# Two small moves on the vector engine in a four-sublayer encoder trunk: the second copy of a gate row, and two gated products

## The chip, the cores and the metric

One NeuronCore of one Trainium2 chip. The time is the device time of one execution in microseconds (us). The kernel before has a median of 1330.57 us over three runs (1330.4 to 1330.78). The engines that matter here: TensorE (PE, matmuls; PEld is its weight load), VectorE (DVE, elementwise work), ScalarE (ACT, copies, casts and activations), GpSimd (POOL, which here issues the DMAs that add into their destination) and the DMA queue that is fed by SyncE (SPq).

## The reference, cut to what matters

Two layers, each of a token mixer and a SwiGLU feed-forward net (FFN), on one sequence of 512 tokens with 1024 features. Every one of the four sublayers has a norm before it and after it, and shift, scale and gate rows from a conditioning vector:

```python
h = rmsnorm(x, norm_g[i, 2]) * (1.0 + scale) + shift
gate, up = jnp.split(h @ w_in, 2, axis=-1)
y = (jax.nn.silu(gate) * up) @ w_out          # w_in 1024 x 5632, w_out 2816 x 1024
x = x + gate_row * rmsnorm(y, norm_g[i, 3])
```

(The last line's `gate_row` is the gate of the conditioning vector, called `gate` in the reference.) All values are float32.

## The kernel before, in words

**Arithmetic.** A float32 operand is split into a high part that TensorE takes in its fp32r format (a cast on ACT) and the remainder (a subtraction on DVE). One product of two tiles is then three matmuls: high by high, high by low and low by high. So every operand tile costs one ACT cast and one DVE subtraction before PE can use it in full.

**Seven products.** The output projection of each FFN is cut into 2 x 2 blocks (tokens in two halves, features in two halves, the inner dimension in even and odd tiles) and computed with seven block products in place of eight; `PRODUCTS` lists for each the result bank (A, B, C, D), the weight block (b11 to b22) and the activation block (a11 to a22, or the sum s1). The sums of weight blocks are made on the way: by DMAs that add (`add_`, issued by POOL) and by DVE. The four results collect in PSUM banks, with A used over and over: when a product has to leave A or has been gathered there, it is copied or combined into an SBUF tile.

**The first FFN** (L1130 to L1271). `seq` lists the steps q; each step is one tile pair of one product: 12 matmuls by `product` (two token tiles x two inner tiles x three). The order on each engine is written out by hand (`manual_schedule`), so an engine takes its instructions in the order of this loop. Behind the matmuls of step q come, in this order: `behind(q)`, which holds copies of finished banks, issues the adding DMAs and makes block differences; then a gate row for q = 0 and 1; then `w_prep(q + 4)`, the split of the weight tile of four steps later (ACT cast L1098, DVE subtraction L1099); then `a_prep(q + 3)`, the split of the activation tile of three steps later (L1107 on ACT, L1108 on DVE) and, for the first two products, one block sum or difference (L1110, L1112). Four weight tiles (`whl_p`) and three activation tiles are in turn.

**Gate rows.** `put_gates(s)` (L310) brings the gate row of sublayer s into DRAM, where the sublayers read it back later, spread over all partitions. It has three steps: a transpose on PE into a PSUM bank `ggp` (L313), a DVE copy of 8 x 128 values into the SBUF tile `gr` (L316), and a DMA of `gr` to `gate_d[s]` on SP's queue (L317). There is a single buffer for `gr`, so a second copy has to wait until the DMA of the first has landed. Rows 2 and 3 are begun together ahead of the step loop (both transposes), and each is finished, copy and DMA, by `list(rows_g[q])` at L1235.

**The last FFN** (L2202 to L2300). The same seven products as 40 steps n. The loop at L2272 runs `products([n])`, then `behind(n)`, then `w_prep(n + 4)` (ACT L1980, DVE L1981) and `a_prep(n + 3)` (ACT L1993, DVE L1994); from n = 34 on, `behind(n)` comes after the two preps. Steps 33 and 27 are run inside the turn of 32 and 26, between `behind(32)` and `behind(33)`, and ahead of the preps. `got["11", t]` is the finished first accumulator (token tile t = 0, 1, first 512 features). Its squares are summed on ACT at n = 29 and 30. `behind(33)` subtracts bank A into `got["22", t]` (L2246), after which A is free for step 34. `behind(34)` takes the square root (ACT, L2215), the reciprocal (DVE, L2216) and multiplies `got["11", t]` by the gate row `gg[0]` (DVE, `gated`, L2219), for t = 0 and 1. `behind(35)` and `behind(36)` do more gated products and write the first outputs (`x_new`, L2225). The last three steps, 37 to 39, run as one group by token tile, and the tail of the kernel squares, gates and writes what is left in bank A. The gate rows `gg` are fetched from `gate_d` at n = 26 (L2283).

Of the kernel before, what the change touches and what calls it, by code (L numbers as in the profile page):

```python
# [38 lines left out]
def trunk_kernel(  # L39
# [540 lines left out]
    with ExitStack() as ph:  # L580
# [571 lines left out]
        with tc.manual_schedule(engines={PE_ENGINE, mybir.EngineType.SP, mybir.EngineType.Activation,  # L1152
                                         mybir.EngineType.DVE, mybir.EngineType.Pool}):
            load_pair(0)
            madds = ada_begin(14)
            for i, f in ((0, 0), (2, 0), (1, 1), (3, 1), (4, 2), (5, 3)):
                rest(i)
                if i in (2, 3):
                    up(f, lead_ps[i])
                    sums(1)  # L1160
                    low_parts()
                else:
                    gate(f, lead_ps[i])
                sums(1)
            finish = out_begin(1, w2, lambda k: acts[k], NF, ggs, xn_lead, "aux", None,
                               lambda: load_w([(wm_in, P, P)]), ys=ys, held=held)[2]
            plain_tiles = finish(())
            tiles = []
            last = 2 * NF - 7
            for k in range(last + 1):  # L1170
                if k % 2 == 0 and k < 2 * NF - 10:
                    load_pair(k // 2 + 1)
                if k in (16, 20, 24):
                    x_load((k - 16) // 4)
                if k in (last - 2, last - 1):
                    xy_load(n_s - 2 + k - last + 2)
                tiles.append(in_chunk(ws[k], h))
                for step in todo:
                    next(step, None)
                q, j = divmod(k - 3, 4)  # L1180
                if j < 2 and k > 2:
                    gate(4 + 2 * q + j, tiles[k - 1])
                elif k:
                    up(2 + 2 * q + j, tiles[k - 1])
                if k + 2 < len(splits):
                    for op in splits[k + 2]:
                        op()
                low_parts()
                sums(4 if j < 2 else 3)
                if k == 2 * NF - 12:  # L1190
                    ggs.append(make_gg(1, gg_tile))
                if k == last - 1:
                    assert next(madds, None) is None and not ada_sets and not quarters
                    sums_p.close()
                    ph.enter_context(tc.tile_pool(name="gap", bufs=1, side="right", reuse_waits="tile")).tile(
                        [P, 216], F32, tag="gap", name="gap")
                    ao_p.append(ph.enter_context(tc.tile_pool(name="aop", bufs=3, side="right", reuse_waits="tile")))
                    ao_p[0].tile([P, 2, 2, 256], F32R, tag="ao", name="ao")
                    gotp = ph.enter_context(tc.tile_pool(name="gotp", bufs=1, side="right", reuse_waits="tile"))
                    c22 = gotp.tile([P, 2, T], F32, tag="c22", name="c22")  # L1200
                if k >= last - 1:
                    w_prep(seq[k - last + 1])
                    a_prep(seq[k - last + 1])
            w_prep(seq[2])
            a_prep(seq[2])
            up(NF - 1, tiles[-1])
            for step in todo:
                list(step)
            rows_g = [put_gates(q, mm_ps) for q in (2, 3)]
            for step in rows_g:  # L1210
                next(step)
            for p in range(n_s - 2):
                y_load(p)
            for p in range(n_s):
                add_(b_("b12", p), b_("b11", p))
            w_prep(seq[3])
            low_parts()
            leads, lead_ops, tail_w = [], [], [[], []]
            tails = ((0, NF - 2), (1, NF - 4), (1, NF - 2))

            def tail_split(i):
                hf, k0 = tails[i]
                w = whl_p.tile([P, 2, 2, T], F32R, tag="whl", name="whlo")
                split_w(plain[hf, k0], w, 2)
                tail_w[hf] += [(k0 + kk, w, kk) for kk in range(2)]

            for q, item in enumerate(seq):
                if item[0] == "s":
                    product(item)
                else:  # L1230
                    w = w_of[item]
                    plain_tiles(item[1], [(item[2] + kk, w, kk) for kk in range(2)], item[3])
                behind(q)
                if q < 2:
                    list(rows_g[q])  # L1235
                if q == 13:
                    plain[1, NS] = plain_load(1, NS, flat_half(s1t, 0))
                    plain[0, NS] = plain_load(0, NS, flat_half(s1t, 1))
                elif q == 24:
                    plain[0, NS + 2] = plain_load(0, NS + 2, flat_half(wx[0], 0))  # L1240
                if q + 4 < len(seq):
                    w_prep(seq[q + 4])
                if q + 3 < len(seq):
                    a_prep(seq[q + 3])
                if q == 27:
                    st_p.close()
                    lead_p.append(ph.enter_context(tc.tile_pool(name="leadp", bufs=16, reuse_waits="tile")))
                    xns += [tile4l([P, 2, T], F32, "xn") for _ in range(4)]
                    for load in ssd_lead[:2]:
                        leads += load(lead_ops)  # L1250
                    for xn, (hf, k0) in zip(xns, tails):
                        plain[hf, k0] = plain_load(hf, k0, xn)
                    for op in lead_ops[:4]:
                        op()
                    leads += ssd_lead[2](lead_ops)
                elif q == 28:
                    for op in lead_ops[4:6]:
                        op()
                    tail_split(0)
                    for op in lead_ops[6:8]:  # L1260
                        op()
                elif q == 29:
                    tail_split(1)
                elif q == 30:
                    tail_split(2)
                    for op in lead_ops[8:10]:
                        op()
                elif q == 31:
                    for op in lead_ops[10:]:
                        op()  # L1270
            begun = finish(tail_w, leads)  # L1271
# [496 lines left out]
    with ExitStack() as ph:  # L1768
# [249 lines left out]
        with tc.manual_schedule(engines={PE_ENGINE, mybir.EngineType.SP, mybir.EngineType.Activation,  # L2018
# [187 lines left out]
            got = {}  # L2206
# [21 lines left out]
            def behind(n):  # L2228

                for t in range(2):  # L2230
                    if n == 5:
                        got["11", t] = t2("c11")
                        act.copy(got["11", t], bank["A"][t])
                    elif n == 10:
                        dve.tensor_add(got["11", t], got["11", t], bank["B"][t])
                    elif n == 16:
                        got["12", t] = t2("c12")
                        act.copy(got["12", t], bank["C"][t])
                    elif n == 21:
                        dve.tensor_add(got["12", t], got["12", t], bank["D"][t])  # L2240
                        got["22", t] = spare[f"c22_{t}"]
                        act.copy(got["22", t], bank["D"][t])
                    elif n == 27:
                        dve.tensor_tensor(got["12", t], got["12", t], bank["A"][t], SUB)
                    elif n == 33:
                        dve.tensor_tensor(got["22", t], got["22", t], bank["A"][t], SUB)  # L2246
                    elif n in (29, 30):
                        if t == n - 29:
                            square(t, 0, got["11", t])
                            square(t, 1, got["12", t])  # L2250
                            mean(t)
                    elif n == 34:
                        root(t)
                        gated(got["11", t], 0, got["11", t])
                    elif n == 35:
                        square(2 + t, 0, got["22", t])
                        mean(2 + t)
                        gated(got["12", t], 1, got["12", t])
                        x_new(t, 0, got["11", t])
                    elif n == 36:  # L2260
                        gated(got["22", t], 1, got["22", t])
                        x_new(t, 1, got["12", t])
# [67 lines left out]
```

## Time and profile before

| | us |
|---|---|
| median of three runs | 1330.57 (1330.4 to 1330.78) |
| the profiled execution's own time | 1330.71 |
| its span, first to last instruction | 1328.9 |
| PE busy, of the span | 1314.1 (99%) |
| DVE busy | 1028.2 (77%) |
| ACT busy | 641.7 (48%) |
| POOL busy | 86.1 (6%) |

The profile's times count from the start of the span. A line of the timeline gives the start, the duration, the engine, the line in the kernel, the operation, what it writes and reads, how many were merged, and in square brackets how long the engine sat idle before it and what ended that idle time. A line of the chain of waits gives start, duration and the engine or transfer on which the end of the kernel hung during that stretch. Instructions of one engine overlap slightly: the next one can begin some 0.1 us before the recorded end of the one before.

### The profile page before, as it was taken

The numbers are of one execution on the slowest core, as the hardware profiler recorded it, in microseconds if no ns is written. First come the engines' busy times: TensorE is split into PE (matmuls) and PEld (weight loads), VectorE is DVE, ScalarE is ACT, GpSimd is POOL, SyncE is SP. The second block draws the span as 40 slices with busy tenths as digits, with TensorE's granted clock in tenths as the row PEclk, the third lists the DMA queues.
The fourth block names the chain that finished last, engine by engine and source line by source line (L and its number), as shares of the span: only waits on it lengthen the run. The fifth ranks groups of instructions, "written<-read, shape, count | busy, mean of one in ns | idle before, by whom it ended". The sixth has DMA issues, their size and how long they took to land.

```text
span 1328.9 us, 19226 instructions
## 1 busy us (share of the span) xinstructions
PE 1314.1 (99%) x7437; PEld 1134.3 (85%) x7437; DVE 1028.2 (77%) x1654; ACT 641.7 (48%) x1042; POOL 86.1 (6%) x106
## 2 busy tenths in 40 slices
PE   8999999999999999999999999999999999999997
PEld 6788889888888788898888888888789999998886
DVE  5588866787776596768998989888677777766897
ACT  5332256222223465665654555554574555554665
POOL 0000000000000140000000000000000111101320
PEclk9999999999999999999999999999999999999999
DMA  9767760788886692414533243413251788869861
GB/s 308 231 193 225 246 229 1 218 265 258 289 285 201 175 171 61 139 34 130 166 121 124 84 138 115 143 64 127 80 158 45 192 216 214 199 191 287 175 124 64
DMA packets 203456, 222.21 MB, mean 167 GB/s; under 512 B 8788, under 2 KB 148964, under 8 KB 202340
## 3 DMA queue, kind: packets, MB, share of 16 engines
q1 hardware_dynamic: 186496, 184.74, 44.7%
q0 software_dynamic: 12720, 23.34, 10.2%
q10 hardware_dynamic: 4148, 12.90, 3.0%
q8 instruction: 58, 0.95, 0.3%
q14 instruction: 34, 0.28, 0.1%
HBM read 195.37 MB, written 2.24 MB: 149 GB/s over the span
## 4 chain that ended last, share of the span: by engine, by line
PE 94%; SPq 2%; DVE 2%; ACT 1%; DMA 1%; issue 1%; DVEq 0%; ACTq 0%
PE ip L279 15%; PE ip L281 14%; PE ip L280 14%; PE y L381 10%; PE sA L1920 7%; PE cA L2015 4%; PE sC L1920 3%; PE cA L1127 3%; PE li L279 3%; PE li L281 3%; PE li L280 3%; PE sB L1920 2%; PE li L767 1%; PE yd L1512 1%; PE cC L2015 1%; PE cB L2015 1%
## 5 line engine op out<-in xcount | busy, mean ns | idle before, releaser
L279 PE MATMUL ip<-h,whl 128*128 128x512 f32 x840 | 331.2, 394 | 0.2 <-DVE cv L874 0.2
L281 PE MATMUL ip<-h,whl 128*128 128x512 f32 x840 | 327.2, 390 | 0.0
L280 PE MATMUL ip<-h,whl 128*128 128x512 f32 x840 | 327.0, 389 | 0.0
L279 PEld LDWEIGHTS ip<-h,whl 128*128 128x128 f32 x840 | 157.8, 188 | 33.8 <-issue 1.8
L281 PEld LDWEIGHTS ip<-h,whl 128*128 128x128 f32 x840 | 157.7, 188 | 33.2
L280 PEld LDWEIGHTS ip<-h,whl 128*128 128x128 f32 x840 | 157.8, 188 | 31.6
L225 DVE TENSOR_TENSOR whl<-wst,whl 128x1024 fp32r<-128x1024 f32 x99 | 120.4, 1221 | 42.2 <-ACT whl L224 42.1
L224 ACT CAST whl<-wst 128x1024 fp32r<-128x1024 f32 x99 | 102.4, 1042 | 57.8 <-DMA wst<-in_f_w_in_dram 47.5
L127 DVE SCALAR_TENSOR_TENSOR ada_acc<-ada_st,csil,ada_acc 128x512 f32<-128x512 f32 x140 | 105.0, 750 | 20.4 <-DMA ada_st<-in_ada_w_dram 17.0
L381 PE MATMUL y<-whlo,ys 128*128 128x512 f32 x384 | 89.4, 392 | 0.0
L381 PEld LDWEIGHTS y<-whlo,ys 128*128 128x128 f32 x384 | 71.7, 188 | 15.9 <-issue 0.7
L279 PE MATMUL li<-h,whl 128*128 128x256 f32 x288 | 83.2, 289 | 0.0
L281 PE MATMUL li<-h,whl 128*128 128x256 f32 x288 | 81.5, 283 | 0.0
L280 PE MATMUL li<-h,whl 128*128 128x256 f32 x288 | 81.5, 283 | 0.0
L1920 PE MATMUL sA<-tq,whl 128*128 128x256 f32 x576 | 74.6, 283 | 0.3 <-DVE g L1946 0.3
L1920 PEld LDWEIGHTS sA<-tq,whl 128*128 128x128 f32 x576 | 71.5, 190 | 0.6 <-DVE g L1946 0.5
L1366 DVE SCALAR_TENSOR_TENSOR cu<-ip,cols,cu 128x511 f32<-128x511 f32 (+2 forms) x84 | 62.7, 747 | 4.0 <-ACT cu L1363 1.4
L2015 PE MATMUL cA<-whlo,ao 128*128 128x512 f32 x264 | 61.2, 390 | 0.8 <-DVE ao L1994 0.4
L2015 PEld LDWEIGHTS cA<-whlo,ao 128*128 128x128 f32 x264 | 49.3, 188 | 12.2 <-ACT whlo L1980 1.2
L1876 DVE TENSOR_TENSOR whl<-wsu,whl 128x1024 fp32r<-128x1024 f32 x33 | 40.4, 1223 | 23.4 <-ACT whl L1875 23.4
L279 PEld LDWEIGHTS li<-h,whl 128*128 128x128 f32 x288 | 55.2, 192 | 0.0
L280 PEld LDWEIGHTS li<-h,whl 128*128 128x128 f32 x288 | 55.2, 192 | 0.0
(371 smaller groups left out, 2319.1 us busy)
## 6 DMA issues: line engine op xcount, KB each, us to landing
ada_st<-in_ada_w_dram SPq DMA_DIRECT2D x96, 512.0 KB, 5.6
wst<-in_f_w_in_dram SPq DMA_DIRECT2D x26, 1024.0 KB, 7.6
wst<-in_m_w_in_dram SPq DMA_DIRECT2D x14, 1024.0 KB, 5.3
wst<-in_m_w_in_dram SPq DMA_DIRECT2D x20, 512.0 KB, 5.7
wst<-in_a_w_in_dram SPq DMA_DIRECT2D x9, 1024.0 KB, 6.9
wsu<-in_f_w_in_dram SPq DMA_DIRECT2D x17, 512.0 KB, 6.0
csb<-cs_d ACTq DMA_DIRECT2D x8, 1024.0 KB, 5.5
sg<-in_f_w_in_dram SPq DMA_DIRECT2D x32, 256.0 KB, 3.3
```

The source lines that it names most:

```text
L127: dve.scalar_tensor_tensor(acc, w, csil[:, k:k + 1], acc, MUL, ADD)
L224: later.append((lambda sw=sw, w=w: act.copy(w[:, 0, :nk, :], sw), lambda sw=sw, w=w: dve.tensor_tensor(w[:, 1, :nk, :], sw, w[:, 0, :nk, : ...
L225: lambda sw=sw, w=w: dve.tensor_tensor(w[:, 1, :nk, :], sw, w[:, 0, :nk, :].bitcast(F32), SUB)))
L279: pe.matmul(dst, w_at(w, 0, kk), a[:, 0, sl], start=start, stop=False)
L280: pe.matmul(dst, w_at(w, 0, kk), a[:, 1, sl], start=False, stop=False)
L281: pe.matmul(dst, w_at(w, 1, kk), a[:, 0, sl], start=False, stop=stop)
L381: pe.matmul(pst, a[:, al, tk], wt[:, wl, kk, :], start=k == 0 and i == 0, stop=k == K - 1 and i == 2, skip_group_check=bool(held))
L1127: pe.matmul(bank[r, sub], a[:, al, q, tk], w[:, wl, q, :], start=first and k == 0, stop=False, skip_group_check=True)
L1366: dve.scalar_tensor_tensor(u[:, sft:], pst[:, :T - sft], w[3 - sft], u[:, sft:], MUL, ADD)
L1876: dve.tensor_tensor(dst[:, 1], src, dst[:, 0].bitcast(F32), SUB)
L1920: pe.matmul(dst, w[:, wl, k0 + k, :], moving(q, k, al), skip_group_check=True, start=q in ("P1", "P5", "P2") and k == 0 and i == 0, stop=k ...
L2015: pe.matmul(bank[r][sub], a[:, al, q, tk], w[:, hl, q, :], start=first and k == 0, stop=last and k == 2, skip_group_check=True)
```

## The change

Two edits, which touch no operand and no result. In the first FFN the second gate row (copy L316 and DMA L317 of row 3) is finished behind step q = 5 in place of q = 1. In the last FFN the two gated products of the first accumulator are issued at n = 31 in place of n = 34; the square roots and reciprocals stay at n = 34.

```diff
@@ first FFN, step loop
                 behind(q)
-                if q < 2:
-                    list(rows_g[q])
+                if q in (0, 5):
+                    list(rows_g[q // 5])
@@ last FFN, behind(n)
                             mean(t)
+                    elif n == 31:
+                        gated(got["11", t], 0, got["11", t])
                     elif n == 34:
                         root(t)
-                        gated(got["11", t], 0, got["11", t])
```

On DVE's instruction stream, row 3's copy (L316) moves from ahead of `w_prep(5)` to ahead of `w_prep(9)`; fourteen DVE instructions lie between. Its DMA keeps its place in SP's queue: no other DMA of that queue lies between the two places. The two products (L2219) move from behind `a_prep(37)` to between `a_prep(33)` (L1994, 128 x 256) and the subtraction of `w_prep(35)` (L1981, 128 x 1024), which is ahead of the two subtractions that free bank A (L2246). Nothing else changes place on any engine. DVE carries out the same number of instructions as before. Of the lines named here only those from L2254 on get other numbers (one more); L2219 and L2246 keep theirs.

## The prediction

> **What bounds the kernel now.** I read the page's table of engines and its chain first, then the chain of waits in order of time around the two places of the change, then the timeline of both places.
>
> ```profile
> PE 94%; SPq 2%; DVE 2%; ACT 1%; DMA 1%; issue 1%; DVEq 0%; ACTq 0%
> ```
>
> The end hangs on PE for 94% of the span. An edit on DVE can only be worth what it does to the few stretches where PE waits. The chain has such a stretch in each of the two places. In the first FFN it reads:
>
> ```profile
> 451.34 2.75 PE cA L1127 x12
> ...
> 456.99 5.35 DMA gate_d<-gr
> 462.36 0.28 DVE gr L316
> 462.64 1.13 DVE whlo L1099
> 463.77 0.61 DVE ao L1108
> 464.43 10.72 PE cB L1127 x46
> 475.15 10.88 PE cC L1127 x48
> ```
>
> The chain leaves PE for the DMA of gate row 2, goes on over the DVE copy of row 3 that waited for it, and comes back to PE by the activation split of step 4. The size of the hole comes from the rate: four steps of 12 matmuls take 10.88 us (the cC row; 0.2267 each). Step 0 began at 451.34, so C should begin 2 x 10.88 later, at 473.10; it begins at 475.15. **PE loses 2.05 us.** The timeline of DVE and ACT there:
>
> ```profile
> 456.88 1.06 ACT L1098 CAST whlo<-w2x 128x1024 fp32r<-128x1024 f32 x1
> 457.85 0.61 ACT L1107 CAST ao<-raw 128x512 fp32r<-128x512 f32 x1
> 458.73 0.69 DVE L1110 TENSOR_TENSOR raw<-s1t,raw 128x512 f32<-128x512 f32 x1
> ...
> 462.36 0.28 DVE L316 COPY gr<-ggp 8x128 f32<-8x128 f32 x1 [2.94 <-DMA gate_d<-gr]
> 462.57 1.20 DVE L1099 TENSOR_TENSOR whlo<-w2x,whlo 128x1024 fp32r<-128x1024 f32 x1
> 463.70 0.67 DVE L1108 TENSOR_TENSOR ao<-raw,ao 128x512 fp32r<-128x512 f32 x1
> ```
>
> DVE sits idle for 2.94 us until the 4 KB of row 2 have landed, although its next split (weight tile 5, L1099) has had its ACT cast since 457.94 and the one after (L1108) since 458.46. PE's first two matmuls of step 4 use high parts only; the third needs that L1108, and waits.
>
> In the last FFN the timeline shows the end of the loop:
>
> ```profile
> 1302.76 0.42 DVE L1994 TENSOR_TENSOR ao<-raw,ao 128x256 fp32r<-128x256 f32 x1
> 1303.10 1.22 DVE L1981 TENSOR_TENSOR whlo<-w2t,whlo 128x1024 fp32r<-128x1024 f32 x1
> 1304.24 0.68 DVE L1994 TENSOR_TENSOR ao<-raw,ao 128x512 fp32r<-128x512 f32 x1
> ...
> 1305.25 1.37 DVE L2246 TENSOR_TENSOR w2h<-w2h,cA 128x512 f32<-128x512 f32 x2 [0.33 <-PE cA L2015]
> ...
> 1306.08 11.62 PE L2015 MATMUL cA<-whlo,ao 128*128 128x512 f32 x50 [0.19 <-DVE w2h L2246]
> ...
> 1309.12 1.15 ACT L1980 CAST whlo<-w2h 128x512 fp32r<-128x512 f32 x2 [1.32 <-PE cA L2015]
> ...
> 1310.81 1.28 ACT L2215 ACT_TABLE_LOAD   x1
> ...
> 1312.10 0.48 ACT L2215 ACTIVATE ss<-ss 128x1 f32<-128x1 f32 x2
> 1312.43 0.17 DVE L2216 RECIPROCAL ss<-ss 128x1 f32<-128x1 f32 x1 [0.40 <-ACT ss L2215]
> 1312.49 0.61 ACT L1980 CAST whlo<-w2h 128x512 fp32r<-128x512 f32 x1
> 1312.51 0.67 DVE L2219 TENSOR_TENSOR c<-c,w2h 128x512 f32<-128x512 f32 x1
> ...
> 1313.10 0.15 DVE L2216 RECIPROCAL ss<-ss 128x1 f32<-128x1 f32 x1
> 1313.17 0.67 DVE L2219 TENSOR_TENSOR c<-c,w2h 128x512 f32<-128x512 f32 x1
> ...
> 1313.76 0.68 DVE L1981 TENSOR_TENSOR whlo<-w2h,whlo 128x512 fp32r<-128x512 f32 x1
> ...
> 1317.62 0.41 DVE L1994 TENSOR_TENSOR ao<-raw,ao 128x256 fp32r<-128x256 f32 x1
> ...
> 1318.09 3.94 PE L2015 MATMUL cA<-whlo,ao 128*128 128x512 f32 x16 [0.39 <-DVE ao L1994]
> ```
>
> PE waits twice: for L2246, which frees bank A for step 34 (1306.08), and for the last activation split (L1994 at 1317.62). By the rate, 50 matmuls from 1306.08 end at 1306.08 + 11.33 = 1317.41, and the next starts at 1318.09: **0.68 us** lost. The two products that move (L2219) lie on DVE ahead of this second wait, and their new place is ahead of the first one.
>
> **The first edit, step by step.** What goes is the 2.94 us wait and the copy. DVE then takes weight tile 5 right behind L1110, at 459.42 (458.73 + 0.69) at the latest; L1099 takes 1.13 to the next start (462.57 to 463.70), so L1108 begins at 460.55 and is done by 461.22. PE's third matmul of step 4 is due at 462.22 + 0.45 = 462.67 (451.34 + 10.88, and two matmuls). So the split is 1.4 us early, and the whole 2.05 goes: **-2.05 us**. What is late next? Nothing at once: a step asks DVE for a weight split (1.13), an activation split (0.67) and a block sum or difference like L1110 (0.69), 2.5 us against PE's 2.72, so the lead grows; the ACT casts of later weight tiles wait for PE to free their buffers and come with it.
>
> What is added, with the next item of SP's queue behind row 3's DMA:
>
> ```profile
> 485.93 5.83 SPq L1083 DMA_DIRECT2D s1t<-in_f_w_out_dram  x2
> ```
>
> The copy comes four steps of 2.5 us behind 459.42, at about 469, and takes 0.21 start to start (462.36 to 462.57) where DVE is ahead by at least that 1.4; the cover gone, it would cost 0.21. It still waits for the DMA of row 2, landed by 462.34, seven us before. The DMA of row 3 goes out about 7 us later than now, 16 us ahead of SP's next item; its reader is in the last FFN (below). I take 0 for copy and DMA.
>
> Weighed against it: the Trainium skill, DMA: Bandwidth & Descriptors, section "Latency and other measured facts", speaks of a DMA's fixed cost of about 2 us. By that alone, an estimate, row 2 would land at 458.99, before DVE could ask, and there would be no wait to remove. This trace differs: 5.35 us.
>
> **The second edit.** Its added part first. In the new place there are two products of 0.59 each from start to next start (1312.51 to 1313.10, 1313.17 to 1313.76): 1.18 us in all, ahead of L1981 at 1303.10. Their gate row is there:
>
> ```profile
> 1263.31 1.10 SPq L2283 DMA_DIRECT2D w2h<-gate_d  x2
> w2h<-gate_d SPq DMA_DIRECT2D x2, 256.0 KB, 4.8
> ```
>
> That is landed by 1270. The only slack up to L2246 is from 1304.84 (L1994 at 1304.24 and 0.60 to the next start) to 1305.25: 0.41. So L2246 comes 1.18 - 0.41 = **0.77 us later**, and PE starts step 34 at 1306.85. Wholly beside other work the pair would cost 0, without slack 1.18; I take 0.77 since both ends of the slack are rows.
>
> Then what it gives back. ACT's casts at 1309.12 wait for PE's step 34, so they, the table load and the square roots behind them all come 0.77 later: roots at 1312.87, first reciprocal at 1313.20, second at about 1313.4, behind the second root's end. The next subtraction (L1981, now 1313.76) needs the cast that moves from 1312.49 to 1313.26 and ends at 1313.87: it starts at about 1313.90. So the 1.18 us taken off DVE here turn into waits for ACT, and the last split comes 0.14 **later**, at 1317.76. PE reaches that point at 1306.85 + 11.33 = 1318.18, and resumes when the split lets it, at 1318.23 in place of 1318.09; everything behind (squares, root, products, the outputs) hangs on this: **+0.14 us**. The bounds: -0.68, the second wait gone and the first not grown; +0.77, nothing given back.
>
> **Sum.** -2.05 + 0.14 = -1.91 us. Against the profiled execution: span 1328.9 to 1326.99, with 1330.71 - 1328.9 = 1.81 around it 1328.80. That execution lies 0.14 above the median, so I take the change from the median: 1330.57 - 1.91 = **1328.7 us**.
>
> **Rivals.**
>
> ```profile
> 1301.62 1.23 DVE L1981 TENSOR_TENSOR whlo<-w2t,whlo 128x1024 fp32r<-128x1024 f32 x1 [1.49 <-ACT whlo L1980]
> ```
>
> *The pair finds room.* If L2246 isn't held up (DVE and PE meet differently at step 33), the second wait goes: -2.05 - 0.68 gives 1327.8. For it: 0.41 of slack and 1.49 us of DVE idle just before 1301.62. Against it: that idle time lies ahead of the pair's place in DVE's order.
>
> *The tail pays in full.* The 0.77 at step 34 stays: -2.05 + 0.77 gives 1329.3. For it: ACT's chain moves with PE. Against it: the 0.68 us hole is there to take it up.
>
> *The first edit doesn't do what it says.* Row 2's DMA is slow only in the profiled execution, and lands ahead of 459.42 in the timed runs, which then have no wait to lose: +0.14 alone, 1330.7. Against it: the profiled execution is 0.14 us, not 2, above the median.
>
> *Starved adds (slower).* In the first FFN, POOL issues the adding DMAs while DVE works:
>
> ```profile
> 462.75 0.86 POOL L1046 DMA_DIRECT2D w2y<-w2x  x1 [1.34 <-DVE gr L316]
> 463.57 0.92 POOL L1046 DMA_DIRECT2D w2s<-w2s  x1
> 464.91 0.87 POOL L1046 DMA_DIRECT2D w2s<-w2s  x1 [0.41 <-issue]
> ...
> 478.56 1.29 DVE L1099 TENSOR_TENSOR whlo<-w2y,whlo 128x512 fp32r<-128x512 f32 x2 [0.52 <-ACT whlo L1098]
> ...
> 480.38 0.68 DVE L1150 TENSOR_TENSOR w2x<-w2y,w2x 128x512 f32<-128x512 f32 x1
> w2y<-w2y POOLq DMA_DIRECT2D x6, 256.0 KB, 4.3
> ```
>
> Three of them were issued from 462.75 on, right as DVE's idle time ended. If POOL can't issue while DVE is busy, they wait for DVE's next hole, the 0.52 us at 478.04, with the new lead 475.99; at 1.34 us each (463.57 to 464.91) the second series starts at 480.0 and its first add lands at about 484.4 (4.3 by the last row). L1150, which reads it, would be due at 478.33: 6.1 late, less the 1.4 of lead 4.7 of PE's time, so 1328.7 + 4.7 = 1333.4. The result is slower than before once that add lands after 481.6 (478.33 + 1.4 + 1.91). Against it: the issues at 463.57 and 464.91 ran beside back-to-back DVE work. By the Trainium skill, SBUF — State Buffer, section "Who interferes with whom", a DVE instruction with two SBUF inputs blocks a GpSimd instruction that reads SBUF, which would speak for this rival; it infers that making descriptors isn't of that kind, and these rows agree.
>
> **How the numbers follow.** Chances: the forecast (1328.3 to 1329.1) 0.63, the pair finds room 0.13, the tail pays in full 0.12, no wait in the timed runs 0.05, starved adds 0.05, else 0.02. 0.2% is 2.66 us, about what a measurement of this kernel can tell from no change: faster is below 1327.91, slower above 1333.23. Faster holds most of the first rival: 0.13. Slower holds most of the starved adds and part of the rest: 0.05. Same: 0.82. The range from 1327.7 to 1329.8 takes in the three likeliest cases.
>
> **What would show it.** Right: no wait of L316 on the DMA; step 4's third matmul directly behind its second, C beginning 10.88 after B; L2246 some 0.77 later against PE's step 33, so that its 0.33 us of idle time is gone; PE's start of step 34 as much later; the hole before the last 16 matmuls gone. Wrong: a new wait in steps 5 to 20 on an adding DMA, on L1099 or L1108; or L2246 not late.

## The result, and the profile after

The kernel after takes 1328.68 us (median of 16 runs, 1328.27 to 1329.71) against 1330.64 us for the kernel before, run beside it (16 runs). The ratio is 0.9984 with a 95% interval of 0.9977 to 0.9992, so the change is faster by 0.16%, inside the bound of 0.2%. The profiled execution took 1328.93 us with a span of 1327.1. Two of those 16 runs of the kernel before took over 1332 us, and in the three sets of runs taken beside the experiments up to nearly half did (its medians there: 1331.03, 1331.64 and 1331.45), so ratios of different sets are not set against each other; what lies behind this is followed below. One run of the experiments took 1446.76 us at a granted clock of 0.85, where all others have 0.996 or more, and is left out.

The chain of waits of the kernel after in the first FFN (start, duration, engine):

```profile
451.31 10.90 PE cA L1127 x48
462.21 10.88 PE cB L1127 x48
473.09 7.03 PE cC L1127 x31
```

No transfer and no vector instruction stands in the chain any more. B begins 10.90 behind A, and C 10.88 behind B: the 2.05 us are gone. The timeline of DVE in the same stretch shows why:

```profile
458.70 0.69 DVE L1110 TENSOR_TENSOR raw<-s1t,raw 128x512 f32<-128x512 f32 x1
459.31 1.22 DVE L1099 TENSOR_TENSOR whlo<-w2x,whlo 128x1024 fp32r<-128x1024 f32 x1
460.44 0.68 DVE L1108 TENSOR_TENSOR ao<-raw,ao 128x512 fp32r<-128x512 f32 x1
...
469.30 0.27 DVE L316 COPY gr<-ggp 8x128 f32<-8x128 f32 x1
```

The split of step 4 (L1108) starts at 460.44 in place of 463.70, and the copy of row 3 at 469.30 has no brackets behind it: it waits for nothing. POOL's timeline, on which the rival of the starved adds rested:

```profile
462.67 0.86 POOL L1046 DMA_DIRECT2D w2y<-w2x  x1 [0.87 <-DMA gate_d<-gr]
463.62 0.86 POOL L1046 DMA_DIRECT2D w2s<-w2s  x1
464.96 0.87 POOL L1046 DMA_DIRECT2D w2s<-w2s  x1 [0.48 <-DVE whlo L1099]
```

The three adds go out at the times of before (462.75, 463.57, 464.91), although DVE now works through the whole stretch. The end of the last FFN, all engines:

```profile
1299.70 1.23 DVE L1981 TENSOR_TENSOR whlo<-w2t,whlo 128x1024 fp32r<-128x1024 f32 x1 [1.49 <-ACT whlo L1980]
...
1300.84 0.42 DVE L1994 TENSOR_TENSOR ao<-raw,ao 128x256 fp32r<-128x256 f32 x1
...
1301.17 1.29 DVE L2219 TENSOR_TENSOR c<-c,w2h 128x512 f32<-128x512 f32 x2
1302.38 1.22 DVE L1981 TENSOR_TENSOR whlo<-w2t,whlo 128x1024 fp32r<-128x1024 f32 x1
...
1304.11 1.28 DVE L2246 TENSOR_TENSOR w2h<-w2h,cA 128x512 f32<-128x512 f32 x2
...
1304.94 15.30 PE L2015 MATMUL cA<-whlo,ao 128*128 128x512 f32 x66 [0.99 <-ACT whlo L1980]
...
1311.30 0.35 DVE L2216 RECIPROCAL ss<-ss 128x1 f32<-128x1 f32 x2 [0.48 <-ACT ss L2215]
...
1311.99 0.69 DVE L1981 TENSOR_TENSOR whlo<-w2h,whlo 128x512 fp32r<-128x512 f32 x1 [0.34 <-ACT whlo L1980]
...
1315.85 0.42 DVE L1994 TENSOR_TENSOR ao<-raw,ao 128x256 fp32r<-128x256 f32 x1
...
1320.28 0.60 ACT L2209 ACTIVATE w2s<-cA 128x512 f32<-128x512 f32 x1 [2.35 <-PE cA L2015]
```

L1994 at 1300.84 stood at 1302.76 before, so this stretch arrives 1.92 us earlier. L2246 stood at 1305.25 and now stands at 1304.11, only 1.14 earlier: the pair ahead of it has cost it 0.78, and its 0.33 us of idle time is used up. PE's 66 matmuls run in one piece, without the hole ahead of the last 16. The profile puts PE's 0.99 us down to an ACT cast; what came last is L2246, whose start lies 0.83 ahead of PE's, as before (1305.25 and 1306.08).

### The profile page after: what moved, and what is told of

The parts are those of the page before. It is cut to its first block, busy times and chain, and to the rows that moved or that the text cites. A ratio compares the mean times of both kernels' runs of the same rounds, so it can differ in the third digit from the quotient of the medians.

```text
span 1327.1 us, 19226 instructions
## 1 busy us (share of the span) xinstructions
PE 1313.8 (99%) x7437; PEld 1134.4 (85%) x7437; DVE 1028.0 (77%) x1654; ACT 641.5 (48%) x1042; POOL 85.9 (6%) x106
## 4 chain that ended last, share of the span: by engine, by line
PE 93%; DMA 2%; SPq 2%; DVE 1%; ACT 1%; issue 1%; DVEq 0%; ACTq 0%
PE ip L279 15%; PE ip L281 14%; PE ip L280 14%; PE y L381 8%; PE sA L1920 7%; PE cA L2015 4%; PE cA L1127 3%; PE sC L1920 3%; PE li L279 3%; PE li L281 3%; PE li L280 3%; PE sB L1920 2%; PE li L767 1%; PE yd L1512 1%; PE cC L2015 1%; PE cD L2015 1%
```

## The experiments

Two theories stood against each other for the first edit. Mine: the wait for the buffer `gr` is the hole. The rival: the hole comes from the place of the copy (the load on DVE in these steps), or is worth something else in the timed runs than in the profile. For the second edit, mine: the pair delays the freeing of bank A by as much as it later frees DVE; the rival: it finds room. Ratios are to the kernel before, run beside each. Since A begins between 450.9 and 452.6 us in different executions, profiles are compared by one distance: from the start of bank A's matmuls in the first FFN to the start of the last square (L2209) in the tail. It is 870.73 us before (the square starts at 1322.07) and 868.97 after. For the second edit a shorter one leaves out what happens ahead of the last FFN: from the weight split of step 34 (L1981, at 1301.62 before and 1299.70 after) to the same square. It is 20.45 us before and 20.58 after.

**The copy alone.** The second hunk of the diff is left out.

> The first edit alone, everything else as before. Theory (the copy's wait for row 2's DMA is the hole in PE; the pair at step 31 costs a little): 2.05 us off, less 0.1 lost again on the way to the end, so 1.9 to 2.05 below the kernel before, about 1328.6; the copy of row 3 at about 469.3 without a wait; cC begins at 473.1; in the last FFN everything stands as before against PE's steps. Rival (the pair finds room, and the first edit is worth less): only 1.2 to 1.4 below, about 1329.3.

Measured: 1328.49 us, ratio 0.9979 (0.9970 to 0.9988); the distance is 868.73, 2.00 less than before, and the shorter distance 20.46 (from 1300.46). Its tail, all engines:

```profile
1304.10 1.37 DVE L2246 TENSOR_TENSOR w2h<-w2h,cA 128x512 f32<-128x512 f32 x2 [0.33 <-PE cA L2015]
...
1304.93 11.60 PE L2015 MATMUL cA<-whlo,ao 128*128 128x512 f32 x50 [0.20 <-DVE w2h L2246]
...
1316.92 3.96 PE L2015 MATMUL cA<-whlo,ao 128*128 128x512 f32 x16 [0.39 <-DVE ao L1994]
```

The two waits of PE stand where they stood before (50 matmuls, a hole, 16). The first edit carries the whole gain.

**The pair alone.** The first hunk is left out.

> The second edit alone. Theory: DVE's L2246 comes 0.77 us later, PE's last 16 matmuls no longer wait, and the end comes 0.14 us later: 1330.8, not to be told from no change by time, but by the rows (L2246 at 1306.0 in place of 1305.25, the last 16 matmuls at about 1318.2). Rival (the pair finds room): 0.68 us earlier, about 1329.9.

Measured: 1331.97 us (median of ten runs), ratio 1.0002 (0.9993 to 1.0011); the distance is 870.97, 0.24 more than before, and the shorter distance 20.57 (from 1301.67), 0.12 more. The tail:

```profile
1306.09 1.27 DVE L2246 TENSOR_TENSOR w2h<-w2h,cA 128x512 f32<-128x512 f32 x2
...
1306.92 15.28 PE L2015 MATMUL cA<-whlo,ao 128*128 128x512 f32 x66 [0.98 <-ACT whlo L1980]
...
1313.24 0.35 DVE L2216 RECIPROCAL ss<-ss 128x1 f32<-128x1 f32 x2 [0.46 <-ACT ss L2215]
...
1317.81 0.41 DVE L1994 TENSOR_TENSOR ao<-raw,ao 128x256 fp32r<-128x256 f32 x1
```

Step 34 starts 0.84 later than before (1306.08), of which 0.05 lies ahead of the pair (L1981 at 1301.67 in place of 1301.62); the hole ahead of the last 16 is gone, and the last split comes at 1317.81 where it came at 1317.62. One wait has become the other.

**The copy at its old place, in a buffer of its own.**

```diff
-        gr = tmp.tile([KD, P], F32, tag="gr", name="gr", bufs=1)
+        gr = tmp.tile([P, 256], F32, tag="uh", name="gr", bufs=2)[:KD, :P] if s == 3 else tmp.tile([KD, P], F32, tag="gr", name="gr", bufs=1)
```

> The kernel before with a second buffer for the gate row (row 3 goes into a tile of another tag that is idle then), both copies in their old places at steps 0 and 1. Theory (the wait for the DMA costs, not the copy's place): the copy of row 3 runs at about 459.3 without a wait, takes its 0.2 us out of the 1.4 us of lead, and PE loses nothing: about 2.0 below the kernel before, 1328.6. Rival (the place counts: DVE work at step 1 is on PE's path): at most the wait less 0.2 and whatever the DMA of row 3 so close behind row 2's adds, 1.5 or less gained, 1329.1 or more.

Measured: 1328.31 us, ratio 0.9980 (0.9971 to 0.9989), distance 868.68. DVE's timeline:

```profile
458.94 0.27 DVE L316 COPY gr<-ggp 8x128 f32<-8x128 f32 x1
```

The copy lies at its old place and waits for nothing, and the gain is that of the copy moved (868.73). So it is the wait for the single buffer, not the copy's place or its 0.21 us.

**The copy behind step 2** (the kernel after, with `q in (0, 2)` in place of `(0, 5)`).

> The changed kernel with row 3 finished behind step 2 in place of step 5. Theory (a wait on the DMA costs PE only what goes beyond DVE's lead): DVE comes to the copy at about 461.8 and waits 0.6 us for row 2 to land (462.34); with the copy 0.8 us of the lead of 1.8 us at step 5 are used, and PE loses nothing: 1328.7 as the changed kernel, cC at 10.88 behind cB. In executions in which row 2 lands 2 us later, about 1 us would come through: a second group of times near 1329.7. Rival (any wait of DVE here goes through to PE): 0.6 to 0.8 above the changed kernel, 1329.4, in every execution.

Measured: 1328.60 us, ratio 0.9977 (0.9968 to 0.9986), distance 868.88. DVE's timeline, and then the chain of waits:

```profile
462.36 0.28 DVE L316 COPY gr<-ggp 8x128 f32<-8x128 f32 x1 [0.61 <-DMA gate_d<-gr]
```

```profile
462.10 10.88 PE cB L1127 x48
472.98 7.03 PE cC L1127 x31
```

DVE still waits 0.61 us for the same landing, and PE loses nothing: DVE's lead over PE covers it. What counts is that the wait no longer stands ahead of step 4's split. Of the second group near 1329.7 that was expected for late landings, there is one run of 11 (1329.56), too few to tell.

**The pair one step earlier, behind step 30** (with the copy moved).

```diff
-                    elif n == 31:
-                        gated(got["11", t], 0, got["11", t])
+                        if n == 30:
+                            gated(got["11", t], 0, got["11", t])
```

> The changed kernel with the two gated products behind step 30, ahead of the split of step 34's weights, where DVE is idle for 1.49 us. Theory (the pair costs only where DVE has no slack): the hole takes the 1.18 us, L2246 stands as before against PE's step 33, the last split comes about 0.63 us earlier (from there ACT's cast of step 39's weights limits), PE's wait before the last 16 matmuls goes: 0.6 to 0.8 below the changed kernel, about 1328.0. Rival (the last split hangs on something else, such as ACT's square roots): no better than the changed kernel's 1328.7.

Measured: 1327.71 us, ratio 0.9970 (0.9960 to 0.9981), distance 868.03, 0.70 less than with the copy alone, and the shorter distance 19.80 (from 1299.27), 0.66 less. This is the fastest of all the kernels here. Its timeline:

```profile
1297.64 0.68 DVE L2219 TENSOR_TENSOR c<-c,w2h 128x512 f32<-128x512 f32 x1
...
1298.30 0.68 DVE L2219 TENSOR_TENSOR c<-c,w2h 128x512 f32<-128x512 f32 x1
...
1299.27 1.23 DVE L1981 TENSOR_TENSOR whlo<-w2t,whlo 128x1024 fp32r<-128x1024 f32 x1 [0.28 <-ACT whlo L1980]
...
1302.89 1.37 DVE L2246 TENSOR_TENSOR w2h<-w2h,cA 128x512 f32<-128x512 f32 x2 [0.32 <-PE cA L2015]
...
1303.72 15.31 PE L2015 MATMUL cA<-whlo,ao 128*128 128x512 f32 x66 [0.19 <-DVE w2h L2246]
```

Here the pair lies ahead of DVE's 1.49 us of idle time, which takes it up: 0.28 is left of it. L2246 keeps its 0.32 us of idle time, so bank A comes free on time, and the 66 matmuls have no hole: the rival "the pair finds room" is right one step earlier, at the prediction's price of 0.68.

**The pair right behind L2246**, inside `behind(33)` (with the copy moved).

> The changed kernel with the two gated products right behind step 33's subtractions (after L2246, ahead of the split of step 36's weights). Theory (the pair costs where it stands ahead of something that PE waits for): L2246 and the start of step 34 as before against step 33, then 1.18 us on DVE ahead of the activation split of step 35, which PE needs about 0.3 us sooner than it comes; the last split some 0.45 us earlier than before. Net 0.4 below the kernel before in this stretch: 1328.3, between the changed kernel and the one with the pair behind step 30. Rival (only the place relative to L2246 counts): the same as behind step 30, 1327.8.

Measured: 1328.38 us, ratio 0.9975 (0.9965 to 0.9986), distance 868.55, 0.18 less than with the copy alone, and the shorter distance 20.21 (from 1300.89), 0.25 less: less than the 0.4 that was expected. The timeline:

```profile
1304.53 1.37 DVE L2246 TENSOR_TENSOR w2h<-w2h,cA 128x512 f32<-128x512 f32 x2 [0.34 <-PE cA L2015]
...
1305.36 15.70 PE L2015 MATMUL cA<-whlo,ao 128*128 128x512 f32 x66 [0.19 <-DVE w2h L2246]
...
1305.81 1.29 DVE L2219 TENSOR_TENSOR c<-c,w2h 128x512 f32<-128x512 f32 x2
...
1308.22 0.68 DVE L1994 TENSOR_TENSOR ao<-raw,ao 128x512 fp32r<-128x512 f32 x1
```

Bank A comes free on time, but the 66 matmuls take 15.70 where they take 15.31 behind the pair of step 30: 0.39 of the 0.68 is lost within them. Matmul by matmul, the trace has the loss at the third and fourth of step 35: the third, the first to need the low part of its activations, starts 0.31 late at 1308.96, right behind their split (L1994 at 1308.22, for 0.68), and the fourth 0.11 more. That is the split that the expectation named.

**The landing without traffic.** Row 3 in its own buffer, its DMA ordered behind step 19, with a DVE write to the buffer behind it, which would have to wait for the landing.

> A measurement, not a candidate: two buffers as in the kernel with two rows, both copies at steps 0 and 1, but the DMA of row 3 is issued behind step 19, where the DMA engines are idle (none of their time is used from 500 to 505), and DVE clears the row's tile right behind, so that its wait is the DMA's time to landing. Theory (row 2 takes 5.4 us or more because the queue's 16 engines are full from 450 to 462): the same 4 KB land in about 2 us there, DVE waits 2 us. Rival (a write of this shape to DRAM takes 5 us wherever it is): DVE waits 5 us.

Measured: 1327.80 us, a single run. The DMA went out at 489.3, since SP isn't held back to DVE's step, and the write that was to wait came 17 us later:

```profile
506.71 0.17 DVE L321 MEMSET gr<- 8x128 f32 x1
```

It waited for nothing, and at 489.3 the DMA engines were not yet idle, so this run has no landing in a quiet stretch. The DMA packets of the traces still tell the two theories apart; neither holds as it stands (last section).

**The kernel before again,** three more profiled executions, each with its expectation.

> The kernel before once more, for its profile: its times come in two groups, 1330.4 to 1331.0 and 1331.7 to 1332.8, while kernels that don't wait at step 1 have hardly any of the upper group. Theory (row 2's DMA lands later in the upper group): in an execution of that group DVE's wait at step 1 is about 2 us longer than 2.94 and cC begins at 477. Rival (something else, ahead of this place or behind it, is longer): the wait is 2.9 in both.

> As the run ahead of it: the kernel before, one more profile, to have both groups of times. Theory: the wait at step 1 goes with the time of the execution. Rival: it doesn't.

> The kernel before a third time, for its profile: row 2 landed 5.35, 5.60 and 6.42 us after its issue in executions of 1330.71, 1330.55 and 1331.5 us. Theory: the time follows the landing; an execution of 1332 us or more shows 7 us or more, PE's hole 3.5 us or more. Rival: it shows 5.5 us and the rest elsewhere.

Measured: 1331.50, 1330.55 and 1332.35 us. The chain of waits of the first (the landing, then what follows):

```profile
456.70 6.42 DMA gate_d<-gr
...
465.22 10.74 PE cB L1127 x46
```

and of the third:

```profile
456.79 5.60 DMA gate_d<-gr
...
464.49 12.34 PE cB L1127 x46
```

The landing varies, and PE pays for it one for one: 5.35 us with a distance of 870.73, 5.60 with 870.95 (the second), 6.42 with 871.81. My guess that the longest executions are those with the latest landing fell with the third: landing 5.60, distance 872.56. Its 46 matmuls take 12.34 us where they take 10.72 elsewhere. The busy times by windows of the third (window; busy time of PE, PEld, DVE, ACT, POOL; granted clock; DMA share; GB/s):

```profile
462.00:465.50 3.50, 1.50 (x7) 0.93 (x6) 3.05 (x5) 2.14 (x4) 2.34 (x3) 1.00 0.86 148
465.50:466.00 0.50, 0.50 (x4) 0.38 (x3) 0.50 (x1) 0.00 (x0) 0.28 (x1) 0.96 0.83 131
466.00:469.00 3.00, 3.00 (x9) 2.33 (x8) 2.97 (x6) 1.06 (x3) 0.00 (x0) 0.50 0.94 160
469.00:469.50 0.50, 0.50 (x3) 0.41 (x2) 0.47 (x2) 0.50 (x2) 0.00 (x0) 0.63 0.00 0
469.50:472.00 2.50, 2.50 (x13) 2.06 (x12) 2.46 (x5) 0.67 (x3) 0.84 (x2) 1.00 0.00 0
```

The granted clock falls to half just behind the hole: 9 matmuls in 3 us where 15 fit elsewhere. That led to the last two kernels.

**The hole filled with matmuls.** The kernel before, with idle work on PE in the place of the hole:

```diff
+                    if r == "B" and first and sub == 0:
+                        for _ in range(9):
+                            pe.matmul(bank[r, sub], a[:, 0, q, tk], w[:, 0, q, :], start=True,
+                                      stop=True, skip_group_check=True)
```

> The kernel before, with nine matmuls more ahead of step 4's first one in the first FFN (high by high parts of that step, into bank B, which the real first matmul then starts anew): 9 x 0.2267 = 2.04 us of PE work in the place of the hole; DVE's wait for the 4 KB of row 2 stays. Both theories expect C to begin where it does before, some 23.8 us after A's start (before 475.15 - 451.34 = 23.81), and so about 1330.6 us in the undisturbed runs. The theory that PE's idle hole is what lets the clock fall to half in some executions expects no run at 1331.5 us or above, where the kernel before had 24 of 63 so far. The rival, that the upper times come from something else in this stretch (the landing of row 2, the wait of DVE), expects about as many of them as the kernel before has in the same call.

> As the kernel with nine more matmuls, but with four: 4 x 0.2267 = 0.91 us of the hole is filled and PE still sits idle for about 1.1 us before step 4's third matmul. C begins 23.81 us after A's start as before, undisturbed runs at about 1330.6 us. If a hole of about 1.1 us is enough to let the clock fall, some runs stand at 1331.5 us or above as with the kernel before; if it has to be nearer to 2 us, none does.

Measured: nine matmuls 1330.90 us, ratio 0.9995 (0.9986 to 1.0004), distance 870.78; four 1330.74 us, ratio 0.9990 (0.9981 to 0.9999), distance 871.08 with a landing of 5.74. The chain of waits with nine:

```profile
450.95 10.89 PE cA L1131 x48
461.85 2.04 PE cB L1128 x9
463.89 10.88 PE cB L1131 x48
474.77 10.88 PE cC L1131 x48
```

PE is never idle here, and C begins 23.82 us behind A, as before (23.81): the time of the hole is set by DVE's wait, whatever PE does meanwhile. Runs at least 1.2 us above the fastest of the same kernel were 1 of 11 with nine matmuls and 2 of 11 with four, beside 10 of 21 of the kernel before, run beside them. (At 1331.5 us, where the expectation forecast none with nine, they are 1, 1 and 10.) Over all sets of runs they were 36 of 84 for the kernel before, 5 of 10 for the pair alone, which keeps the wait, and 6 of 64 for the six kernels without the hole. So they come with PE's idle hole, and filling it takes most of them away although DVE's wait stays. The fall of the clock itself was seen in one profile, but each run has its mean granted clock on record, which 3.41 us at half (last section) would lower by 0.0013. Of 69 runs of the kernel before, the 30 above 1331.9 us have 0.996 to 0.998, but for one at 0.999; the other 39 have 0.998 or 0.999. The longest run with nine matmuls (1332.03) and with four (1331.54) stand at 0.999, so nothing there points to a fall. Whether 1.23 us of idle time, as with four, is always harmless, eleven runs don't settle.

## Why the prediction was right, step by step

- **The hole of 2.05 us goes.** Right: it went by 2.03 (C at 473.09 where 475.15 less 0.03 of an earlier start was due), and by 2.00 and 2.05 in the distances of the two kernels that only take the wait away. That the wait for `gr` is its whole cause is shown by the copy in its own buffer at the old place.
- **L1099 at 459.42 at the latest, L1108 at 460.55, the copy at about 469.** They came at 459.31, 460.44 and 469.30.
- **L2246 0.77 later, PE's step 34 as much.** 0.78 against the 1.92 by which the stretch is early; for PE, 1306.08 less 1.92 is 1304.16, and it starts at 1304.94, 0.78 later.
- **What DVE gets back turns into waits for ACT, and the last split comes 0.14 later.** The reciprocals wait 0.48 for the square roots, the next subtraction 0.34 for its cast, and the split at 1315.85 is 0.15 late (1317.62 less 1.92 is 1315.70). By the shorter distance the pair costs 0.12, both on top of the copy (20.58 less 20.46) and alone (20.57 less 20.45): the term of +0.14 was right. By the long one it is 0.24 each time; the other half lies ahead of the last FFN, where the pair can't act: in the transposes of the next point, and for the pair alone about half of it in row 2's landing (5.40 us in place of 5.35).
- **The sum of -1.91.** The medians differ by 1.96, the distances by 1.76. That the median of 1328.68 stands 0.02 from the forecast is luck in part: the interval of the ratio alone is 2.0 us wide. Of the 0.15 that is missing in the profile, 0.10 is one place that neither edit touches: the first transposes ahead of the last FFN (L502, four matmuls) take 0.54 us where they take 0.44 before and with the copy alone (and 0.56 with the pair behind L2246), and the lead falls there from 2.04 to 1.95.
- **Rivals.** The starved adds fall: POOL's issues keep their times. No wait in the timed runs falls: the timed runs gained 1.96, the profile 1.76. The tail paying in full falls: the hole ahead of the last 16 took up the delay. The pair finding room falls at step 31 and holds at step 30.
- **What was not in the prediction:** the hole can cost more than its own length, since the clock can fall behind it. In the runs of the result that shows in 2 of 16 runs of the kernel before and hardly moves its median; where it shows in half of them, taking the wait away alone gained 0.20 to 0.21%, beside the 0.16% of the whole change here.

## What to carry to other kernels

A small copy into a single buffer, issued in order on a busy engine, makes everything behind it wait for the landing of the DMA before it; a second buffer, or a place a few steps later, takes the wait away, and either is worth the hole on PE, and what the clock loses behind it. Before moving work off a late stretch, look for the engine's idle time and put the work ahead of it: two 0.59 us products cost 0.12 us right behind 1.49 us of idle time and gained 0.66 one step earlier, ahead of it. Compare parts of a change by a distance between two events of the same execution, and keep it short: starts that differ by 1.6 us hide effects of this size, and over the long distance 0.1 us came from places that no edit touches.

## What the runs showed of the hardware

**The granted clock behind a short hole.** In one of four profiled executions of the kernel before, the clock fell to half after PE had been idle for 2.00 us (462.49 to 464.49). From the windows above, it was at half from about 465.96 (0.96 over 0.5 us is 0.04 us at half) to 469.37 (0.63 over 0.5 us is 0.37 at half): 3.41 us, worth 12.34 - 10.72 = 1.6 us. A hole of 2.82 us in another execution (landing 6.42) left it at 1.00. The clock records of the traces suggest why. In the thirteen other executions the clock, once full, stays so for 1314.13, 1317.55 or 1320.96 us, which are 385, 386 and 387 times 3.413; in the one with the fall it is full for 457.39 (134 times), at half for 3.41 and full for 856.75 (251 times). So it changes at steps of 3.41 us, and where these lie against the kernel differs: the clock first goes full between 5.97 and 9.23 us. Laid over PE's idle time, one such step holds 1.94 us of the hole where the clock fell. The hole of 2.82 is cut by an edge, with 1.87 in one step; the other two executions have 1.85 and 0.91 at most. That a step must be idle for about 1.9 us is a guess from one fall, not shown. The Trainium skill, TensorE: Matmul & The Clock Gate, section "What's actually happening", has the clock at either half or full, set by a free-running window of 3413 ns: the half, the 3.41 us and the chance character agree with it. The Trainium skill, TensorE: Matmul & The Clock Gate, section "HAM oscillation — how this bites in real kernels", asks for no idle gaps above about 3.4 us; by these rows 2.0 us can be enough, and the rows decide.

**4 KB that take 5 to 6 us.** The copy of row 2 lands 5.35, 5.40, 5.60, 5.60, 5.74 and 6.42 us after its issue in six of the executions that have the wait. While it is under way, the 16 DMA engines are full. Two windows of the kernel before, and one of the kernel after while row 3 is written (last two columns: DMA share, GB/s):

```profile
457.00:459.00 2.00, 2.00 (x11) 1.65 (x10) 1.97 (x3) 1.46 (x2) 0.00 (x0) 1.00 1.11 252
459.00:461.00 2.00, 2.00 (x11) 1.65 (x10) 0.42 (x1) 1.40 (x2) 1.33 (x2) 1.00 1.13 208
469.60:471.60 2.00, 2.00 (x11) 1.65 (x10) 2.00 (x4) 1.20 (x3) 0.96 (x3) 1.00 1.03 174
```

Full engines alone don't make it slow. The traces list the packets of every DMA queue, and the 4 KB are eight packets of 512 bytes. Row 2's in the kernel before run from 3.43 to 4.71 us behind the issue (456.99), and up to then SP's queue still moves packets of the six loads issued on it from 446.39 to 449.79. Row 3's in the kernel after, issued at 469.60 with nothing ahead of it in SP's queue, are through after 2.03 us, with engines about as full (1.03). In the kernel meant for a quiet stretch, row 3's went out 0.42 us behind another load on SP's queue (488.90) and were through after 4.88 us. So the time goes with what stands ahead in the same queue; no run changed that alone, so it is argued from three transfers, not shown.
